# RWKV's triangular inverse with squares moved by transfers alone and masked products, and ScalarE's table set for logarithm and exponential asked for ahead of norms

## The chip, the cores and the metric

The kernel runs on one core of one Trainium2 chip. A core has TensorE (matrix products), VectorE, ScalarE (activations, by function tables that are loaded as sets) and GpSimd as compute engines, each with its own queue of instructions in a fixed order; SyncE (SP) issues most of the DMA transfers. Engines wait for each other by semaphores. The metric is the time of one launch on the device in microseconds.

## The reference

A step of a decoder trunk of two layers, on 512 prompt tokens and 8 x 8 sample tokens, with width 1024. Each layer mixes tokens with four recurrent mixers of four heads each (HGRN2, GLA, RWKV-7, RetNet), gates their results, and adds a gated feed-forward network:

```python
h = RMSNorm(x); P = h @ W_in[l]
o_b = mixer_b(P_b)                     # hg, gl, rw, rt: 256 wide each
x = x + W_out[l](sum_b sigmoid(G_b) * (o_b @ W_branch[l, b]))
x = x + SwiGLU(RMSNorm(x))

def rwkv7_recurrence(r, log_w, k, v, kk, a, s0):
    def step(S, inp):
        kS = jnp.einsum('bhk,bhkv->bhv', kk_t, S)
        S = (jnp.exp(lw_t)[..., None] * S
             - (a_t * kk_t)[..., None] * kS[..., None, :]
             + k_t[..., None] * v_t[..., None, :])
        return S, jnp.einsum('bhk,bhkv->bhv', r_t, S)
```

RMSNorm, the mixers' head norms (`_head_rms`, RWKV's `_head_layernorm` and the normalised `kk`) all need a reciprocal square root.

## The kernel before

Tokens lie along the free axis, 576 of them, worked on as two halves of 288. A weight product is three fp16 matmuls per k tile, high and low parts of both operands (lines 241 to 243, tile `pb`); the weights arrive as float32 and are split by ScalarE (line 228) and VectorE (line 229), 512 columns at a time. The input projection, the mixers and the gates run interleaved: `mix` (line 1623) goes through units of weight products in a hand-made order and advances a Python generator for each mixer at a pace (table `PACE`); a scheduler then fixes the order on each engine from what is ready. TensorE so has weight products beside the chain of small steps of the mixers.

**RWKV.** Nine chunks of 64 tokens are evaluated in closed form. `rwkv_pair` (line 669) works on two of the four heads at once, head pair 0 or 1, so there are two in each layer and four in the run. It makes the triangular matrices of a chunk, products `gps` (line 733) of `rw_br` and `rw_ab` (written at line 723), which VectorE masks into U (`rw_ub`, line 737): 128 partitions (two heads x 64 tokens) by 9 chunks by 128 columns, block diagonal by heads. Meanwhile `bps` (line 754) waits for the bonus term `rn` (line 750).

`rwkv_inverse` (line 894) then inverts the unit triangular I + U:

- GpSimd multiplies U by the constant `diag16` into W, so that only the 16x16 squares on the diagonal remain (line 901), and VectorE adds the eight squares of a row up into a compact `uc` of 16 columns (line 903);
- eight transfers on SP's queue carry `uc` to DRAM (`d1`, line 907), and one brings it back with a square per partition (`pp`, line 909). VectorE inverts the 72 squares by 15 steps of substitution, with a result `wp` that goes to `d2` (line 924) and in eight transfers back to `wc` (line 927);
- VectorE spreads `wc` over W with the mask (line 938). Then, for two groups of four chunks, the blocks of 32 and 64 follow: W is transposed (`itt`, line 946), multiplied by a part of U (`imu`, U masked for the level by line 932; product `ixp`, line 950), copied to SBUF by ScalarE (line 952), multiplied by W (`iyp`, line 960), and subtracted from W by VectorE (line 962).

In the same stretch VectorE runs HGRN2's and GLA's levels: scores of a chunk are built level by level from `lk` (line 1111) and `qt` (line 1122) with TensorE's product `lvp` (line 1026) and a predicated copy (line 1137).

**Reciprocal square roots.** All are made on ScalarE as exp(-0.5 ln(.)). The compiler puts a load of a table set ahead of an activation whose function is not in the set that is loaded. The places are `rstd` (RMSNorm, lines 444 and 445; called by `norm_half`), `head_rms_out` (HGRN2, GLA, RetNet, lines 515 and 516, behind the product `hps`), `rw_gen` (RWKV's norm, lines 657 and 658, behind `vps`) and `rwkv_pair` (the norm of `kk`, lines 694 and 695, behind `kps`). Around them ScalarE computes tanh for gates and sigmoids (lines 498, 630, 1458, 1540), exponentials for decays (line 1110) and silu in the feed-forward (line 1779). A gate's product with its branch is `gu` (line 1550).

Of the kernel before, what the change touches and what calls it, by code (L numbers as in the profile page):

```python
# [62 lines left out]
def host_constants():  # L63

    f = []
# [26 lines left out]
    for m in (16, 32):  # L92
        up = ((s2[:, None] // (2 * m) == s2[None, :] // (2 * m)) & (s2[:, None] // m % 2 == 0)
              & (s2[None, :] // m % 2 == 1)).astype(np.float32) * same
        put(f"rw_l{m}", up)
    put("diag16", (p[:, None] // 16 == p[None, :] // 16).astype(np.float32))
    c = np.arange(128)
# [77 lines left out]
class Net:  # L175
# [250 lines left out]
    def sq_acc(self, k, half, last=False):  # L426
# [8 lines left out]
        elif not last:  # L435
            nc.vector.tensor_tensor(self.acc[half], self.acc[half], sq, op=ADD)

    def rstd(self, half):

        nc = self.nc  # L440
        ps = self.psum("g", [128, HW], "rps")
        nc.tensor.matmul(ps, self.cf("ones"), self.acc[half], start=True, stop=True)
        r = self.t("e", [128, HW], "rstd")
        nc.scalar.activation(r, ps, AF.Ln, scale=1.0 / D, bias=self.eps[:, 0:1])
        nc.scalar.activation(r, r, AF.Exp, scale=-0.5)
        return r

    def norm_half(self, name, l, half, keep=False):


        nc = self.nc
        hs = slice(half * HW, half * HW + HW)
        if half == 0:
            self.h = [self.t("u", [128, 2, T], f"h{k}", F16) for k in range(KT)]
        self.norm_tiles(name, l, half, self.rstd(half), [x[:, hs] for x in self.x], keep)

# [47 lines left out]
    def head_rms_out(self, o, g, wcol, name):  # L504
# [3 lines left out]
        for j in range(2):  # L508
            sq = self.t("gs", [128, T], "hsq")
            nc.scalar.activation(sq, o[j], AF.Square)  # L510
            yield
            for t0, n in ((0, HW), (HW, HW)):
                ps = self.psum("g", [128, n], "hps")
                nc.tensor.matmul(ps, self.cf("head"), sq[:, t0:t0 + n], start=True, stop=True)
                nc.scalar.activation(sq[:, t0:t0 + n], ps, AF.Ln, scale=1.0 / 64, bias=self.eps[:, 0:1])
# [120 lines left out]
    def rw_gen(self, l):  # L636
# [4 lines left out]
        for j in range(2):  # L641
# [6 lines left out]
            for hs in part:  # L648
# [3 lines left out]
                nc.scalar.copy(O[:, hs], ps)  # L652
                yield
            for hs in part:
                ps = self.psum("r", [128, HW], "vps")
                nc.tensor.matmul(ps, self.cf("head"), sq[:, hs], start=True, stop=True)
                nc.scalar.activation(sq[:, hs], ps, AF.Ln, scale=1.0 / 64, bias=self.eps[:, 1:2])
# [11 lines left out]
    def rwkv_pair(self, l, j, lw):  # L669
# [16 lines left out]
        rn = tmp("rn")  # L686
        yield
        for hs in halves:
            ps = self.psum("r", [128, HW], "kps")
# [204 lines left out]
    def rwkv_inverse(self, U):  # L894
# [3 lines left out]
        ub = U.rearrange("p c h s -> p c (h s)")  # L898
        dg = self.cf("diag16").rearrange("p (g t) -> p g t", t=16)
        W = self.t("rd", [128, 9, 128], "rw_w")  # L900
        nc.gpsimd.tensor_tensor(W, ub, self.cf("diag16")[:, None, :].to_broadcast([128, 9, 128]), op=MUL)
        uc = self.t("r2", [128, 9, 16], "rw_uc")
        nc.vector.tensor_reduce(uc, W.rearrange("p c (g t) -> p c t g", t=16), axis=mybir.AxisListType.X, op=ADD)
        d1 = self.dr.tile([8, 9, 16, 16], F32, tag="d1", name="rw_d1")
        d2 = self.dr.tile([8, 9, 16, 16], F32, tag="d2", name="rw_d2")
        for g in range(8):
            nc.sync.dma_start(out=d1[g].rearrange("c s t -> s c t"), in_=uc[16 * g:16 * g + 16])
        pp = self.t("r1", [72, 16, 16], "rw_pp")
# [15 lines left out]
        nc.sync.dma_start(out=d2.rearrange("g c s t -> (g c) s t"), in_=wp)  # L924
        wc = self.t("r2", [128, 9, 16], "rw_wc")
        for g in range(8):
            nc.sync.dma_start(out=wc[16 * g:16 * g + 16], in_=d2[g].rearrange("c s t -> s c t"))
        n = 4

        def part(c0, m):  # L930
            mu = self.t("r2", [128, n, 128], "imu")
            nc.vector.tensor_tensor(mu, ub[:, c0:c0 + n], self.cf(f"rw_l{m}")[:, None, :].to_broadcast([128, n, 128]),
                                    op=MUL)
            return mu
        mu = part(0, 16)
        for _ in range(3):
            yield
        nc.vector.tensor_tensor(W.rearrange("p c (g t) -> p c g t", t=16),
                                wc[:, :, None, :].to_broadcast([128, 9, 8, 16]),
                                dg[:, None].to_broadcast([128, 9, 8, 16]), op=MUL)  # L940
        for c0 in (0, 4):
            w0 = W[:, c0:c0 + n]
            w = w0
            for m in (16, 32):
# [4 lines left out]
                for i in range(n):  # L949
                    nc.tensor.matmul(ps[:, i], mu[:, i], tt[:, i], start=True, stop=True)  # L950
                xx = self.t("r2", [128, n, 128], "ixx")
                nc.scalar.copy(xx, ps)
                if m == 16:
                    mu = part(c0, 32)
                elif c0 == 0:
                    mu = part(4, 16)
                yield
                ps = self.psum("r", [128, n, 128], "iyp")
                for i in range(n):
                    nc.tensor.matmul(ps[:, i], xx[:, i], w[:, i], start=True, stop=True)  # L960
                w2 = self.t("r2", [128, n, 128], "iw") if m == 16 else w0
                nc.vector.tensor_tensor(w2, w, ps, op=SUB)
                w = w2
                yield
# [994 lines left out]
```

## Time and profile before

| | |
|---|---|
| median of 3 runs | 2194.13 us (2193.98 to 2196.09) |
| the profiled execution | 2198.27 us, span 2196.5 us |
| TensorE busy | 2032.3 us |
| VectorE busy | 1622.8 us |
| ScalarE busy | 1080.3 us |
| GpSimd busy | 643.7 us |

The span runs from the first to the last instruction of the profiled execution; its own time adds what lies around it. Busy time does not count waiting. A timeline's row gives start, duration, engine, line, operation, output and inputs, and in brackets the idle time before it with what ended it. Line numbers are those of the kernel before.

### The profile page before, as it was taken

Reading aid. Unit: us, or ns where it says so; the run is one execution under the profiler, and the core shown is the slowest. Engines: PE = TensorE matmul, PEld = TensorE weight load, DVE = VectorE, ACT = ScalarE, POOL = GpSimd, SP = SyncE. Lnnn points to the kernel's source line nnn. Section 1 sums busy time; section 2 is a strip of 40 time slices with the busy share of each in tenths; the row PEclk is TensorE's granted clock in tenths of the full one; section 3 lists DMA queues with packets and bytes.
Section 4 is the critical chain, followed back from the end, with each engine's and each line's share of the span. In section 5 each row is a group of like instructions: output and inputs, shape, how many; then the busy total and the mean of one; then the engine's idle time right before and its main releaser. Section 6 shows DMA issues by size and latency. Waiting matters only on the chain.

```text
span 2196.5 us, 42364 instructions
## 1 busy us (share of the span) xinstructions
PE 2032.3 (93%) x15754; PEld 1608.8 (73%) x15754; DVE 1622.8 (74%) x3409; ACT 1080.3 (49%) x2524; POOL 643.7 (29%) x889
## 2 busy tenths in 40 slices
PE   7989999998998899999999899989999989999998
PEld 5767786786776677777777678768777767777776
DVE  7889667768786899863488986586778778998441
ACT  6554546345555555432466355453645455544332
POOL 2223222146541534310012142213464225332000
PEclk9999999999999999999999999999999999999999
DMA  6312224334545455453421222242354544554431
GB/s 182 84 42 63 59 59 110 78 84 106 132 121 170 101 141 132 111 145 99 125 66 50 55 64 59 74 111 62 85 133 112 154 130 116 136 137 107 125 107 51
DMA packets 381275, 223.75 MB, mean 102 GB/s; under 512 B 60675, under 2 KB 361275, under 8 KB 381069
## 3 DMA queue, kind: packets, MB, share of 16 engines
q1 hardware_dynamic: 365516, 192.73, 31.3%
q0 software_dynamic: 15552, 28.32, 7.4%
q8 instruction: 124, 2.03, 0.4%
q14 instruction: 83, 0.67, 0.1%
HBM read 173.72 MB, written 16.59 MB: 87 GB/s over the span
## 4 chain that ended last, share of the span: by engine, by line
PE 49%; DVE 25%; ACT 8%; issue 8%; DMA 5%; POOL 3%; SPq 1%; DVEq 0%; ACTq 0%; POOLq 0%
PE pb L243 5%; PE pb L242 5%; PE pb L241 5%; PE xb L243 4%; PE xb L242 4%; PE xb L241 4%; PE fsS L1736 2%; PE fsS L1735 2%; PE fsS L1734 2%; DVE hA L1704 2%; DVE whl L229 2%; DVE fy L1781 2%; DVE hS L1704 2%; DVE sc L1750 2%; DVE su L1750 2%
## 5 line engine op out<-in xcount | busy, mean ns | idle before, releaser
L241 PE MATMUL pb<-h,whl 128*128 128x288 f16 (+1 forms) x1504 | 434.6, 289 | 4.4 <-ACT whl L228 2.1
L243 PE MATMUL pb<-h,whl 128*128 128x288 f16 (+1 forms) x1504 | 434.2, 289 | 3.2 <-DVE whl L229 3.1
L242 PE MATMUL pb<-h,whl 128*128 128x288 f16 (+1 forms) x1504 | 434.6, 289 | 0.6 <-DVE h L465 0.4
L229 DVE SCALAR_TENSOR_TENSOR whl<-raw,whl 128x512 f16<-128x512 f32 (+1 forms) x352 | 253.6, 730 | 130.5 <-ACT whl L228 128.8
L243 PEld LDWEIGHTS <-whl 128*128 128x128 f16 (+1 forms) x2784 | 274.9, 99 | 86.5 <-issue 11.6
L242 PEld LDWEIGHTS <-whl 128*128 128x128 f16 (+1 forms) x2784 | 275.1, 99 | 85.0 <-issue 10.7
L241 PEld LDWEIGHTS <-whl 128*128 128x128 f16 (+1 forms) x2784 | 276.7, 99 | 76.1 <-issue 3.6
L228 ACT ACTIVATE whl<-raw 128x512 f16<-128x512 f32 (+1 forms) x352 | 213.0, 617 | 165.2 <-PE pb L243 50.6
L243 PE MATMUL xb<-fa,whl 128*128 128x288 f16 x704 | 201.3, 286 | 0.0
L242 PE MATMUL xb<-fa,whl 128*128 128x288 f16 x704 | 201.3, 286 | 0.0
L241 PE MATMUL xb<-fa,whl 128*128 128x288 f16 x704 | 201.3, 286 | 0.0
L1734 PE MATMUL fsS<-st,hS 128*128 128x288 f16 x456 | 132.5, 291 | 6.5 <-ACT hS L1703 6.5
L1734 PE MATMUL fsA<-h,hA 128*128 128x288 f16 x432 | 124.2, 288 | 9.4 <-DVE gu L1550 8.4
L1736 PE MATMUL fsS<-st,hS 128*128 128x288 f16 x456 | 132.5, 291 | 0.4 <-DVE hS L1704 0.3
L1735 PE MATMUL fsS<-st,hS 128*128 128x288 f16 x456 | 132.5, 291 | 0.0
L1736 PE MATMUL fsA<-h,hA 128*128 128x288 f16 x432 | 124.3, 288 | 0.2
L1735 PE MATMUL fsA<-h,hA 128*128 128x288 f16 x432 | 124.3, 288 | 0.0
L1703 ACT ACTIVATE hS<-sraw 128x512 f16<-128x512 f32 x130 | 79.8, 623 | 63.6 <-POOL sraw L1718 42.4
L1734 PEld LDWEIGHTS <-hS 128*128 128x128 f16 x864 | 85.5, 99 | 34.6 <-ACT hS L1703 12.6
L1704 DVE SCALAR_TENSOR_TENSOR hS<-sraw,hS 128x512 f16<-128x512 f32 x130 | 103.2, 798 | 9.1 <-ACT hS L1703 8.1
L1736 PEld LDWEIGHTS <-hS 128*128 128x128 f16 x864 | 85.7, 99 | 24.6 <-DVE hS L1704 2.4
L1735 PEld LDWEIGHTS <-hS 128*128 128x128 f16 x864 | 85.6, 99 | 22.8
(489 smaller groups left out, 5207.6 us busy)
## 6 DMA issues: line engine op xcount, KB each, us to landing
raw<-in_w_in SPq DMA_DIRECT2D x208, 256.0 KB
sraw<-in_w_ffn_in SPq DMA_DIRECT2D x40, 512.0 KB
raw<-in_w_ffn_out SPq DMA_DIRECT2D x80, 256.0 KB
raw<-in_w_ffn_in SPq DMA_DIRECT2D x78, 256.0 KB
sraw<-sraw POOLq DMA_DIRECT2D x40, 256.0 KB, 3.7
x<-xd SPq DMA_DIRECT2D x32, 288.0 KB
raw<-sraw POOLq DMA_DIRECT2D x34, 256.0 KB, 3.3
sraw<-in_w_in SPq DMA_DIRECT2D x32, 256.0 KB
```

Source lines behind the costliest of these rows:

```text
L228: nc.scalar.activation(hl[:, 0, :n], raw[:, :n], AF.Copy, scale=WS)
L229: nc.vector.scalar_tensor_tensor(hl[:, 1, :n], raw[:, :n], WS, hl[:, 0, :n], op0=MUL, op1=SUB)
L241: nc.tensor.matmul(ps, wh, hi, start=i == 0, stop=False)
L242: nc.tensor.matmul(ps, wh, lo, start=False, stop=False)
L243: nc.tensor.matmul(ps, wl, hi, start=False, stop=i == len(ks) - 1)
L1703: nc.scalar.activation(hl[:, 0], a, AF.Copy, scale=WS)
L1704: nc.vector.scalar_tensor_tensor(hl[:, 1], a, WS, hl[:, 0], op0=MUL, op1=SUB)
L1734: nc.tensor.matmul(ps, w[a][:, 0, k], hi, start=k == 0, stop=False)
L1735: nc.tensor.matmul(ps, w[a][:, 0, k], lo, start=False, stop=False)
L1736: nc.tensor.matmul(ps, w[a][:, 1, k], hi, start=False, stop=k == 3)
L1750: nc.vector.tensor_tensor(o, a, p, op=op)
L1781: nc.vector.scalar_tensor_tensor(y, u, PH * AS, sg, op0=MUL, op1=MUL)
```

## The change

The inverse. GpSimd fills W with zeros and U isn't masked. The eight transfers to `d1` read the 16x16 squares on U's diagonal from U itself, and the eight from `d2` write the inverted squares onto W's diagonal; `uc`, `wc`, the reduction, the spread and `diag16` go. The products `ixp` take U unmasked, ScalarE's copy negates, and the last product is written into W by a copy that is predicated by the level's mask, in place of masks on U and a subtraction.

The tables. A method `table` asks for a table set at its place in the order, which the scheduler keeps. It asks for the set with both functions ahead of `rstd`'s product, `hps` and `vps`, for the set "natural_log" ahead of `kps`, and behind `rstd` for the set of silu or of exp.

```diff
+    def table(self, name="natural_log_exp_and_others"):
+
+        self.tc.keep_in_program_order(self.nc.scalar.preload_act_table_set(name))
+
     def rstd(self, half):
         ps = self.psum("g", [128, HW], "rps")
+        self.table()
         nc.tensor.matmul(ps, self.cf("ones"), self.acc[half], start=True, stop=True)
...
-        self.norm_tiles(name, l, half, self.rstd(half), [x[:, hs] for x in self.x], keep)
+        r = self.rstd(half)
+        self.table("silu_and_others" if keep else "exp_and_others")
+        self.norm_tiles(name, l, half, r, [x[:, hs] for x in self.x], keep)
...
@@ head_rms_out, for each j, ahead of both hps
+            self.table()
@@ rw_gen, ahead of both vps
+            self.table()
@@ rwkv_pair, ahead of both kps
+        self.table("natural_log")
...
@@ rwkv_inverse
         ub = U.rearrange("p c h s -> p c (h s)")
-        dg = self.cf("diag16").rearrange("p (g t) -> p g t", t=16)
         W = self.t("rd", [128, 9, 128], "rw_w")
-        nc.gpsimd.tensor_tensor(W, ub, self.cf("diag16")[:, None, :].to_broadcast([128, 9, 128]), op=MUL)
-        uc = self.t("r2", [128, 9, 16], "rw_uc")
-        nc.vector.tensor_reduce(uc, W.rearrange("p c (g t) -> p c t g", t=16), axis=mybir.AxisListType.X, op=ADD)
+        nc.gpsimd.memset(W, 0.0)
...
         for g in range(8):
-            nc.sync.dma_start(out=d1[g].rearrange("c s t -> s c t"), in_=uc[16 * g:16 * g + 16])
+            b = slice(16 * g, 16 * g + 16)
+            nc.sync.dma_start(out=d1[g].rearrange("c s t -> s c t"), in_=ub[b, :, b])
...
-        wc = self.t("r2", [128, 9, 16], "rw_wc")
         for g in range(8):
-            nc.sync.dma_start(out=wc[16 * g:16 * g + 16], in_=d2[g].rearrange("c s t -> s c t"))
+            b = slice(16 * g, 16 * g + 16)
+            nc.sync.dma_start(out=W[b, :, b], in_=d2[g].rearrange("c s t -> s c t"))
...
-        def part(c0, m):
-            mu = self.t("r2", [128, n, 128], "imu")
-            nc.vector.tensor_tensor(mu, ub[:, c0:c0 + n], self.cf(f"rw_l{m}")[:, None, :].to_broadcast([128, n, 128]),
-                                    op=MUL)
-            return mu
-        mu = part(0, 16)
         for _ in range(3):
             yield
-        nc.vector.tensor_tensor(W.rearrange("p c (g t) -> p c g t", t=16),
-                                wc[:, :, None, :].to_broadcast([128, 9, 8, 16]),
-                                dg[:, None].to_broadcast([128, 9, 8, 16]), op=MUL)
...
-                    nc.tensor.matmul(ps[:, i], mu[:, i], tt[:, i], start=True, stop=True)
+                    nc.tensor.matmul(ps[:, i], ub[:, c0 + i], tt[:, i], start=True, stop=True)
                 xx = self.t("r2", [128, n, 128], "ixx")
-                nc.scalar.copy(xx, ps)
-                if m == 16:
-                    mu = part(c0, 32)
-                elif c0 == 0:
-                    mu = part(4, 16)
+                nc.scalar.activation(xx, ps, AF.Copy, scale=-1.0)
...
-                w2 = self.t("r2", [128, n, 128], "iw") if m == 16 else w0
-                nc.vector.tensor_tensor(w2, w, ps, op=SUB)
-                w = w2
+                mk = self.cf(f"rw_l{m}").bitcast(I32)
+                nc.vector.copy_predicated(w, mk[:, None, :].to_broadcast([128, n, 128]), ps)
```

What stands where in the built kernels (the changed kernel's own line numbers differ by some 10; `L439` is the method `table`). First VectorE around U of head pair 0 in layer 0, before:

```order
242 L739 TENSOR_TENSOR rw_ar<-gps,cst 128x64
243 L229 SCALAR_TENSOR_TENSOR whl<-raw,whl 128x512
244 L423 SCALAR_TENSOR_TENSOR gl_lg<-cst,gl_lg 128x128 x2
245 L903 TENSOR_REDUCE rw_uc<-rw_w 128x144
246 L1071 TENSOR_TENSOR gs<-gkv,cst 128x256
247 L1107 TENSOR_TENSOR le_2010<-hg_f 128x256
248 L1074 SCALAR_TENSOR_TENSOR gs<-gs,glb 128x128 x2
249 L423 SCALAR_TENSOR_TENSOR gl_lg<-cst,gl_lg 128x128
250 L1111 TENSOR_TENSOR lk_2011<-hg_k,le_2010 128x256
251 L1122 TENSOR_TENSOR qt_568<-hg_q,le_2010 64x2x64 x2
```

and now:

```order
245 L748 TENSOR_TENSOR rw_ar<-gps,cst 128x64
246 L228 SCALAR_TENSOR_TENSOR whl<-raw,whl 128x512
247 L422 SCALAR_TENSOR_TENSOR gl_lg<-cst,gl_lg 128x128 x2
248 L422 SCALAR_TENSOR_TENSOR gl_lg<-cst,gl_lg 128x64
249 L1063 TENSOR_TENSOR gs<-gkv,cst 128x256
250 L1099 TENSOR_TENSOR le_2009<-hg_f 128x256
251 L1066 SCALAR_TENSOR_TENSOR gs<-gs,glb 128x128 x2
252 L1103 TENSOR_TENSOR lk_2010<-hg_k,le_2009 128x256
253 L1114 TENSOR_TENSOR qt_568<-hg_q,le_2009 64x2x64 x2
```

The reduction is gone from ahead of `qt`, one scan of `gl_lg` stands earlier, and two more rows stand ahead of row 245 than ahead of row 242 before: a split of weights and another scan of `gl_lg`.

ScalarE at HGRN2's head norm of layer 0 (`hsq` is what the norm is made of, `le` a decay's exponential, `ixx` a copy in the inverse), before:

```order
235 L515 ACT_TABLE_LOAD
236 L515 ACTIVATE hsq<-hps,eps 128x288 x2
237 L952 COPY ixx<-ixp 128x512
238 L516 ACT_TABLE_LOAD
239 L516 ACTIVATE hsq<-hsq 128x576
240 L1110 ACTIVATE le_2988<-le_2988 128x16x4 x2
241 L515 ACT_TABLE_LOAD
242 L515 ACTIVATE hsq<-hps,eps 128x288 x2
243 L1110 ACT_TABLE_LOAD
244 L1110 ACTIVATE le_3027<-le_3027 128x32x2
245 L516 ACTIVATE hsq<-hsq 128x576
```

and now:

```order
230 L439 ACT_TABLE_LOAD
231 L1102 ACTIVATE le_2921<-le_2921 128x8x8 x2
232 L227 ACTIVATE whl<-raw 128x512
233 L493 ACTIVATE cur<-pb 128x288
234 L439 ACT_TABLE_LOAD
235 L522 ACTIVATE hsq<-hps,eps 128x288 x2
236 L949 ACTIVATE ixx<-ixp 128x512
237 L523 ACTIVATE hsq<-hsq 128x576
238 L227 ACTIVATE whl<-raw 128x512
239 L1102 ACTIVATE le_2977<-le_2977 128x16x4
240 L522 ACTIVATE hsq<-hps,eps 128x288 x2
241 L1102 ACTIVATE le_2977<-le_2977 128x16x4
```

Two loads stand ahead of the first `hsq` from `hps`, none from there to the second.

ScalarE ahead of a gate's tanh (`gth`) in layer 0, now; `kvb` and `rxv` are copies in RWKV:

```order
505 L803 COPY kvb_581<-rw_v 64x64
506 L439 ACT_TABLE_LOAD
507 L1450 ACT_TABLE_LOAD
508 L1450 ACTIVATE gth<-pb 128x288
509 L828 COPY rxv<-xvp 128x256
```

Two loads stand in a row, where one stood ahead of the same tanh (line 1458) before.

## Rows read from the trace of the kernel before

**Rows 1.** busy time of each engine over the whole span, with its instruction count.

```profile
PE 2032.3 (93%) x15754; PEld 1608.8 (73%) x15754; DVE 1622.8 (74%) x3409; ACT 1080.3 (49%) x2524; POOL 643.7 (29%) x889
```

**Rows 2.** shares of the chain of work that ended last.

```profile
PE 49%; DVE 25%; ACT 8%; issue 8%; DMA 5%; POOL 3%; SPq 1%; DVEq 0%; ACTq 0%; POOLq 0%
```

**Rows 3.** what TensorE waited for: total us, times, longest us.

```profile
PE lvp L1026 <- DVE qt L1122: 19.9, 18, 3.6
...
PE gps L733 <- DVE rw_ab L723: 7.6, 2, 4.1
...
PE bps L754 <- DVE rn L750: 6.8, 2, 3.6
...
PE lvp L1026 <- ACT hsq L515: 5.3, 2, 2.6
...
PE fsA L1734 <- DVE gu L1550: 8.4, 6, 2.4
```

**Rows 4.** VectorE in order of time, head pair 0 of layer 0: start, us.

```profile
146.79 3.08 DVE L229 SCALAR_TENSOR_TENSOR whl<-raw,whl 128x512 f16<-128x512 f32 x1
...
150.44 2.05 DVE L903 TENSOR_REDUCE rw_uc<-rw_w 128x144 f32<-128x1152 f32 x1
...
154.25 0.58 DVE L1122 TENSOR_TENSOR qt<-hg_q,le 64x128 f32<-64x128 f32 x2
```

**Rows 5.** TensorE there, and in layer 1; idle time before it in brackets.

```profile
154.98 1.19 PE L1026 MATMUL lvp<-qt,lk 128*128 128x128 f32 x4 [3.63 <-DVE qt L1122]
...
1228.48 0.68 PE L1026 MATMUL lvp<-qt,lk 128*128 128x128 f32 x4 [3.63 <-DVE qt L1122]
```

**Rows 6.** groups by line: busy us in all, mean ns of one.

```profile
L901 POOL TENSOR_TENSOR rw_w<-rw_ub,cst 128x1152 f32<-128x1152 f32 x4 | 11.6, 2894 | 37.3 <-DVE rw_ub L737 37.3
...
L229 DVE SCALAR_TENSOR_TENSOR whl<-raw,whl 128x512 f16<-128x512 f32 x332 | 244.9, 744 | 128.4 <-ACT whl L228 126.7
...
L932 DVE TENSOR_TENSOR imu<-rw_ub,cst 128x512 f32<-128x512 f32 x16 | 11.0, 688 | 3.9 <-PE ixp L950 3.9
...
L938 DVE TENSOR_TENSOR rw_w<-rw_wc,cst 128x1152 f32<-128x1152 f32 x4 | 5.4, 1359 | 0.2 <-issue 0.2
...
L962 DVE TENSOR_TENSOR iw<-rw_w,iyp 128x512 f32<-128x512 f32 x8 | 5.5, 689 | 2.6 <-PE iyp L960 2.6
...
L1137 DVE COPY_PREDICATED sc<-lev,lvp 128x256 f32<-128x256 int32 x112 | 57.8, 516 | 13.7 <-PE lvp L1026 12.9
```

**Rows 7.** stretches: start:end, length, busy us (count) of PE PEld DVE ACT POOL, PEclk.

```profile
133.50:156.00 22.50, 18.18 (x132) 15.06 (x133) 22.02 (x47) 7.60 (x24) 4.83 (x8) 0.89 0.24 61
...
376.00:397.00 21.00, 15.15 (x105) 11.67 (x106) 19.89 (x35) 8.37 (x17) 3.53 (x3) 0.92 0.39 101
...
1291.00:1310.00 19.00, 15.74 (x105) 12.07 (x104) 14.74 (x26) 13.75 (x26) 6.85 (x15) 0.91 0.25 66
...
1448.00:1475.00 27.00, 19.75 (x134) 15.54 (x132) 23.24 (x40) 11.39 (x22) 4.62 (x6) 0.87 0.36 94
```

**Rows 8.** ScalarE in order of time at HGRN2's head norm, layer 0.

```profile
217.50 1.28 ACT L515 ACT_TABLE_LOAD   x1
...
222.47 1.28 ACT L515 ACT_TABLE_LOAD   x1
...
223.76 0.89 ACT L515 ACTIVATE hsq<-hps,eps 128x288 f32<-128x288 f32 x2
...
224.67 1.28 ACT L1110 ACT_TABLE_LOAD   x1
```

**Rows 9.** VectorE in order of time, head pair 1 of layer 0.

```profile
384.82 3.71 DVE L229 SCALAR_TENSOR_TENSOR whl<-raw,whl 128x512 f16<-128x512 f32 x2
...
389.20 2.07 DVE L903 TENSOR_REDUCE rw_uc<-rw_w 128x144 f32<-128x1152 f32 x1
```

**Rows 10.** a GpSimd memset beside VectorE's split, in order of time.

```profile
444.21 0.31 POOL L1160 MEMSET gkh<- 128x256 f32 x1
444.27 0.68 DVE L229 SCALAR_TENSOR_TENSOR whl<-raw,whl 128x512 f16<-128x512 f32 x1
```

More of the change, by code (lines that the diff above doesn't have):

```diff
@@ L95, in host_constants @@
         put(f"rw_l{m}", up)
-    put("diag16", (p[:, None] // 16 == p[None, :] // 16).astype(np.float32))
     c = np.arange(128)
@@ L924, in rwkv_inverse @@
         nc.sync.dma_start(out=d2.rearrange("g c s t -> (g c) s t"), in_=wp)
-        wc = self.t("r2", [128, 9, 16], "rw_wc")
         for g in range(8):
-            nc.sync.dma_start(out=wc[16 * g:16 * g + 16], in_=d2[g].rearrange("c s t -> s c t"))
+            b = slice(16 * g, 16 * g + 16)
+            nc.sync.dma_start(out=W[b, :, b], in_=d2[g].rearrange("c s t -> s c t"))
         n = 4
-        def part(c0, m):
-            mu = self.t("r2", [128, n, 128], "imu")
-            nc.vector.tensor_tensor(mu, ub[:, c0:c0 + n], self.cf(f"rw_l{m}")[:, None, :].to_broadcast([128, n, 128]),
-                                    op=MUL)
-            return mu
-        mu = part(0, 16)
         for _ in range(3):
             yield
-        nc.vector.tensor_tensor(W.rearrange("p c (g t) -> p c g t", t=16),
-                                wc[:, :, None, :].to_broadcast([128, 9, 8, 16]),
-                                dg[:, None].to_broadcast([128, 9, 8, 16]), op=MUL)
         for c0 in (0, 4):
-            w0 = W[:, c0:c0 + n]
-            w = w0
+            w = W[:, c0:c0 + n]
             for m in (16, 32):
```

## The prediction

> **What bounds the kernel now.** I read the busy times first: TensorE works 2032.3 us of a span of 2196.5 us, so all its idle time together is 164.2 us; VectorE is at 74% and ScalarE at 49% [rows 1]. The chain that ended last is half TensorE and a quarter VectorE [rows 2]. So no amount of saved work on VectorE or ScalarE counts by itself: it counts where TensorE stands still for it. The list of TensorE's waits says where that is [rows 3]. Four of its entries hang on work that the change touches: the level products `lvp` that wait for `qt` (19.9 us over 18 waits, two of them 3.6 us), `gps` that waits for `rw_ab` (7.6 us over 2), `bps` that waits for `rn` (6.8 us over 2), and `lvp` behind HGRN2's head norm (5.3 us over 2). Each has one instance per layer, so what is found in layer 0 is counted twice. Last I read those stretches in order of time. In the two RWKV stretches of layer 0, VectorE is busy 22.02 of 22.5 us and 19.89 of 21 us while TensorE is not [rows 7]: there VectorE is the bound, and a microsecond off it is worth up to one.
>
> **The inverse, head pair 0.** GpSimd's masked copy of U takes 2.9 us, four times per run [rows 6]. It does not run beside VectorE for nothing: the split (line 229) that meets it takes 3.08 us where the mean of its form is 0.74 [rows 4, 6], so VectorE loses 2.3 us. The reduction behind it takes 2.05 [rows 4]. Both stand ahead of the `qt` for which TensorE waits 3.63 us in each layer [rows 5]. The change puts a memset for the mask and drops the reduction: 4.4 us off VectorE ahead of that `qt`. The new order lets back in one scan more and moves one split up, which by their durations is about 1 us, so 3.0 of the 3.63 us go: **-6.0 us** for two layers. Between what bounds: nothing (the split is held by the memset as it was by the copy, and the rest moves) and the whole 7.3. For the memset I take no hold at all: a smaller memset of 0.31 us starts 0.06 us ahead of a split that then takes 0.68 us, its normal time [rows 10]. If it held the split through, it would take back at most the 2.3 us above, four times, of which two lie on TensorE's path.
>
> **Behind it in pair 0.** Four masks of 0.69 us and the spread of the squares, 1.36 us, leave VectorE in each inverse [rows 6]: 16 x 0.69 + 4 x 1.36 = 16.4 us in the run, half of it in pair 0, where TensorE waits for VectorE in pieces of 0.6 to 1 us that are part of the 19.9 [rows 3]. I take 1 us per layer: **-2.0 us**, bounds 0 and -4.5. In pair 1 the same work lies beside long matrix products, and I take nothing. The masked product in the subtraction's place is a predicated copy of 128x512. A predicated copy of half that size takes 0.52 us in the mean, a subtraction of the whole size 0.69 [rows 6]; so it costs between 0 and +0.35 us more each, 16 times, half of them in pair 0, and TensorE waits for few of them: bounds 0 to +2, taken as 0. The transfers keep their number, eight out and eight back on SP's queue, and start earlier, with the reduction gone from ahead of them.
>
> **Pair 1.** The same two things stand between `rw_ab` and the `rn` for which `bps` waits: the pair of splits takes 3.71 us where twice 0.74 is normal, and the reduction 2.07 [rows 6, 9]. That is 4.3 us out of VectorE's way, against waits of 6.8 us over the two layers [rows 3], 3.4 each. In the new order one more split stands there, so 3.6 us net: both waits go, **-6.8 us**. Against it: ahead of the same chain ScalarE now loads a table before `rw_sg` and another before `re`. The first falls into time in which ScalarE waits for VectorE, so I cost it at nothing; if that cover is gone it is 1.28 us per layer. The second delays `re`, and with it `rw_ab`, for which TensorE already waits 7.6 us over two layers [rows 3]: 2 x 1.28 = **+2.6 us** [rows 8].
>
> **The tables at the norms.** At HGRN2's head norm ScalarE loads four tables within 9 us, 1.28 us each [rows 8]: logarithm, exponential, logarithm, exponential, while TensorE waits 2.6 us for the second logarithm [rows 3]. In the new order two loads stand there, both before the first logarithm, and none between. The two that go, 2.57 us, cover the wait: **-5.3 us** for two layers, bounds -3 and -5.3 (the extra load for the next tanh comes where ScalarE waits anyway). In the feed-forward norm one load less stands in the second half of each layer, at most 1.28 us each; TensorE's wait there also hangs on VectorE, so I take half, **-1.3 us**. The first half is behind other products, and RetNet's and GLA's norms are not waited for.
>
> **Where loads are added.** By the listings of the two built kernels the change does not lower the count in the whole program: 71 loads against 61, as some of the preloads do not replace a load but precede another one. The added ten are 10 x 1.28 = 12.8 us of ScalarE. Twice per layer a preload stands directly ahead of another load, in front of the tanh of the gates, and TensorE waits for the product of gate and branch (`gu`) 8.4 us in six waits [rows 3]. One of the two pairs per layer I place on that path: **+2.6 us**, bounds 0 and +5.1.
>
> First the row on what a load costs: the logarithm starts at 223.76, 1.29 us after its load started [rows 8], so a load holds ScalarE for its 1.28 us and nothing more. The Trainium skill ("ScalarE: Activation LUTs", What ACT_TABLE_LOAD costs) states 1283 ns and about 1380 ns of drain on top, 2.66 us for a switch. By that, the ten added loads would be 26.6 us of ScalarE, and the forecast some 3 us higher; the trace does not agree on the drain, so I go by the trace.
>
> **The clock.** In the four stretches the granted clock is 0.89, 0.92, 0.91 and 0.87 [rows 7]: it falls to the lower of its two levels (1.2 instead of 2.4 GHz) for some microseconds after TensorE stood still. The loss is 0.11 x 22.5 + 0.08 x 21 + 0.09 x 19 + 0.13 x 27 = 9.4 us. Two of the stretches keep another wait of over 3 us (the earlier `qt`, and `rw_ab`), so I take a third back, **-3.1 us**, bounds 0 and -6.7.
>
> **Sum.** -6.0 - 2.0 - 6.8 + 2.6 - 5.3 - 1.3 + 2.6 - 3.1 = -19.3 us. The profiled execution took 2198.3 us with a span of 2196.5; the median of the runs is 2194.1, 0.2% less. A difference of 19 us is the same for both, so the forecast is 2194.1 - 19.3 = 2175 us, 0.9% less.
>
> **Rivals.** *The waits only move.* VectorE's order around pair 0 is full of work for TensorE; what is taken out lets TensorE reach the next `lvp`, `gop` or `bps` sooner, and it stands there instead. For it: the 18 waits for `qt`, of which only two are the long ones [rows 3]. Against it: in pair 1 TensorE is busy 15.15 of 21 us with weight products that don't wait for the chain [rows 7], so it has work to fill the time with. Then only the head norm's 5.3 us and some 2 of the rest are left, against the +5.2 us of added loads: 2194.1 - 2 = 2192 us. *The table loads decide it.* The point is ScalarE's path to `rw_ab` and to the gates: if it is ScalarE and not VectorE that is late there, then what leaves VectorE in pair 1 is worth nothing and each added load is paid in full, with its place kept by an order that can't move it. Price: 12.8 us for ten loads, less the 5.3 at the head norm and 2 in pair 0: 2194.1 + 5.5 = 2200 us. For it: TensorE already waits for `rw_ab`, and for the gates. Against it: ScalarE is busy only 8.37 of 21 us in pair 1's stretch [rows 7]. *All of it comes.* At the outer bounds -7.3 - 4.5 - 6.8 - 5.3 - 2.6 - 6.7 + 2.6 = -30.6: 2163 us. *The change does not do what it says*: the preloads don't replace loads at all at the head norm, because the compiler puts its own behind them. The listing of the built kernel speaks against it there, and for it at the gates; then 5.3 us less: 2180, inside the forecast's own range.
>
> **How the numbers follow.** The forecast, from 2168 to 2185, has 0.55; all of it, 2160 to 2168, 0.10; less than the forecast but still a gain, 2185 to 2189.7, 0.09; the waits only move, 2190 to 2198, 0.14; the loads decide, above 2198.5, 0.12. A difference of 0.2%, 4.4 us, is about what a measurement of this kernel can tell from none. That gives faster 0.74, same 0.14, slower 0.12. The range leaves out the lower half of the full gain and the slower case: 2164 to 2197.
>
> **What would show it.** In the new trace: the split that meets the memset takes about 0.7 us, and no wait of 3.6 us for `qt` stands near 151 or 1225 (pair 0); `bps <- rn` falls from 6.8 to under 1 us, and `gps <- rw_ab` rises from 7.6 to about 10; `lvp <- hsq` is gone; `fsA <- gu` rises from 8.4 to about 11; the granted clock of the stretch at HGRN2's head norm in layer 1 is 1.00. Wrong would be: waits for `qt` that stay at 19.9 us in sum, a split still at 3 us beside the memset, a predicated copy of over 1 us, or a total TensorE idle time near 164 us.

## The result and the profile after

The changed kernel takes 2171.6 us in the median of four runs (2170.0 to 2174.8), the kernel before 2194.9 in the same set. The ratio is 0.9889, with an interval of 0.9877 to 0.9902: 1.1% or 24 us faster. The forecast was 2175 us. The profile after, as its page gives it, the line with the span and the one with the busy times:

```profile
span 2173.0 us, 42394 instructions
...
PE 2028.8 (93%) x15754; PEld 1603.7 (74%) x15754; DVE 1587.5 (73%) x3385; ACT 1089.7 (50%) x2534; POOL 630.3 (29%) x889
```

TensorE's idle time is 2173.0 - 2028.8 = 144.2 us, against 164.2 [rows 1]: 20.0 us less. Its busy time is 3.5 us less with the same number of products, which I put down to the clock (mean granted clock 0.982 against 0.981). Together they are the 23.5 us by which the span is shorter. What TensorE waited for, by the list of its waits (total us, times, longest us), to be set beside [rows 3]:

```profile
PE lvp L1018 <- DVE qt L1114: 10.8, 14, 2.8
PE fsA L1726 <- DVE gu L1542: 10.0, 7, 3.0
PE xvp L825 <- DVE rws L877: 9.0, 6, 3.0
PE gps L742 <- DVE rw_ab L732: 5.4, 2, 2.8
...
PE fb L241 <- POOL h L471: 4.0, 2, 2.0
...
PE xps L859 <- ACT rw_o L831: 3.5, 2, 1.8
...
PE bps L763 <- DVE rn L759: 3.0, 2, 2.3
```

The waits for `qt` fell from 19.9 to 10.8 us, those for `rn` from 6.8 to 3.0. The wait for HGRN2's `hsq`, 5.3 us before, has no row any more. `rw_ab` did not go where the prediction put it: it fell from 7.6 to 5.4. `gu` rose from 8.4 to 10.0, but a second profile of the same kernel (e12 below) has 8.3 for `gu` and 4.5 for `gop` behind `vz`, where this one has 10.0 and 3.1; so a single profile does not show changes of 1 to 2 us in these two entries. The other entries above come back in e12 within 0.6 us. The rows for GpSimd's `h` and for `xps` had no counterpart of that size before.

VectorE behind the last part of U in head pair 0, layer 0, in order of time (start, us), and TensorE's product behind `qt`, to be set beside [rows 4, 5]:

```profile
146.46 0.46 DVE L746 TENSOR_TENSOR rw_ub<-gps,cst 64x64 f32<-64x64 f32 x2
...
147.10 0.68 DVE L228 SCALAR_TENSOR_TENSOR whl<-raw,whl 128x512 f16<-128x512 f32 x1
147.69 0.92 DVE L422 TENSOR_TENSOR_SCAN gl_lg<-cst,gl_lg 128x128 f32<-128x128 f32 x3
...
150.24 0.58 DVE L1114 TENSOR_TENSOR qt<-hg_q,le 64x128 f32<-64x128 f32 x2
```

```profile
150.96 0.68 PE L1018 MATMUL lvp<-qt,lk 128*128 128x128 f32 x4
```

The split takes 0.68 us in place of 3.08, the reduction is gone, `qt` is done by 150.8 where it took until 154.8 before, and the product has no idle time in brackets where it had 3.63. The memset is not even near the split: GpSimd does it 24 us earlier, since it needs nothing of U. So whether it would hold a split that it met was not put to the test here.

```profile
122.88 1.06 POOL L909 MEMSET rw_w<- 128x1152 f32 x1
```

And the group of the predicated copies (busy us in all, mean ns of one) shows 0.73 us for 128x512, against 0.69 of the subtraction [rows 6]:

```profile
L955 DVE COPY_PREDICATED rw_w<-cst,iyp 128x512 f32<-128x512 int32 x16 | 11.6, 726 | 3.9 <-PE iyp L953 3.8
```

ScalarE at HGRN2's head norm, layer 0, in order of time, beside [rows 8]; and the product `lvp` that waited there:

```profile
211.13 1.28 ACT L439 ACT_TABLE_LOAD   x1
...
213.66 1.28 ACT L439 ACT_TABLE_LOAD   x1
214.95 0.89 ACT L522 ACTIVATE hsq<-hps,eps 128x288 f32<-128x288 f32 x2
...
217.48 0.99 ACT L522 ACTIVATE hsq<-hps,eps 128x288 f32<-128x288 f32 x2
```

```profile
218.12 0.67 PE L1018 MATMUL lvp<-qg,lk 128*128 128x256 f32 x2
```

Both loads stand ahead of the first logarithm, and from there to the second there is none. The product starts without idle time. The clock, by stretches that answer to [rows 7] (busy us with counts of PE, PEld, DVE, ACT, POOL, then PEclk):

```profile
133.50:152.00 18.50, 17.53 (x131) 14.62 (x132) 17.54 (x46) 8.12 (x24) 2.88 (x8) 0.91 0.20 47
365.00:388.00 23.00, 18.02 (x129) 14.13 (x127) 18.98 (x39) 9.77 (x21) 2.63 (x7) 0.93 0.35 88
1272.00:1292.00 20.00, 19.11 (x143) 15.40 (x142) 16.10 (x32) 14.71 (x34) 6.85 (x16) 1.00 0.22 59
1430.00:1452.00 22.00, 18.50 (x132) 14.40 (x131) 18.98 (x39) 9.72 (x21) 2.75 (x7) 0.92 0.35 89
```

At the head norm of layer 1 it is 1.00, from 0.91. In pair 1 of layer 1 it is 0.92, from 0.87; in the other two it hardly moved. In e12, the same kernel again, it is 1.00, 0.93, 1.00 and 1.00 in the same four stretches (the last two start some 4 us earlier there): only the second and the third come out alike in both profiles.

### The profile page after: what moved, and what is told of

The parts are those of the page before. It is cut to its first block, busy times and chain, and to the rows that moved or that the text cites. A ratio compares the mean times of both kernels' runs of the same rounds, so it can differ in the third digit from the quotient of the medians.

```text
span 2173.0 us, 42394 instructions
## 1 busy us (share of the span) xinstructions
PE 2028.8 (93%) x15754; PEld 1603.7 (74%) x15754; DVE 1587.5 (73%) x3385; ACT 1089.7 (50%) x2534; POOL 630.3 (29%) x889
## 4 chain that ended last, share of the span: by engine, by line
PE 50%; DVE 22%; ACT 9%; issue 8%; DMA 6%; POOL 2%; SPq 1%; DVEq 0%; ACTq 0%; POOLq 0%
PE pb L242 5%; PE pb L241 5%; PE pb L240 5%; PE xb L241 4%; PE xb L242 4%; PE xb L240 4%; PE fsS L1728 2%; PE fsS L1726 2%; PE fsS L1727 2%; DVE fy L1773 2%; DVE hA L1696 2%; DVE hS L1696 2%; DVE sc L1742 2%; DVE su L1742 2%; PE lvp L1018 2%
## 5 line engine op out<-in xcount | busy, mean ns | idle before, releaser
L228 DVE SCALAR_TENSOR_TENSOR whl<-raw,whl 128x512 f16<-128x512 f32 (+1 forms) x352 | 243.1, 699 | 138.9 <-ACT whl L227 137.0
L1726 PEld LDWEIGHTS <-hS 128*128 128x128 f16 x864 | 85.5, 99 | 34.9 <-ACT hS L1695 12.9
L1696 DVE SCALAR_TENSOR_TENSOR hA<-sraw,hA 128x512 f16<-128x512 f32 x110 | 96.6, 888 | 13.1 <-ACT hA L1695 13.1
L1728 PEld LDWEIGHTS <-hS 128*128 128x128 f16 x864 | 85.3, 99 | 24.8 <-DVE hS L1696 2.4
```

The lines of the kernel that those rows point to most:

```text
L228: nc.vector.scalar_tensor_tensor(hl[:, 1, :n], raw[:, :n], WS, hl[:, 0, :n], op0=MUL, op1=SUB)
L1696: nc.vector.scalar_tensor_tensor(hl[:, 1], a, WS, hl[:, 0], op0=MUL, op1=SUB)
L1726: nc.tensor.matmul(ps, w[a][:, 0, k], hi, start=k == 0, stop=False)
L1728: nc.tensor.matmul(ps, w[a][:, 1, k], hi, start=False, stop=k == 3)
```

## The experiments

e1 to e4 were made on one chip and e5 to e12 on another; the kernel before takes 2200.6 to 2201.5 us beside them. Each is given as its ratio to the kernel before on the same chip, and in us as that share of 2194. "Idle" is the span less TensorE's busy time, from each run's page. The kernel before was profiled only beside the result (idle 164.2 us); e6 and e7, which take as long as it does, have 164.5 and 163.6. Below the overview the runs are grouped by what they ask.

| run | what it is | ratio (95%) | us | idle us |
|---|---|---|---|---|
| the change | | 0.9889 (0.9877 to 0.9902) | -24 | 144.2 |
| e1 | the inverse alone | 0.9942 (0.9922 to 0.9962) | -13 | 155.4 |
| e2 | all table requests alone | 0.9963 (0.9949 to 0.9977) | -8 | 151.0 |
| e3 | the change, GpSimd's mask kept | 0.9919 (0.9896 to 0.9942) | -18 | 146.7 |
| e4 | the change, a reduction kept | 0.9890 (0.9870 to 0.9910) | -24 | 143.3 |
| e5 | HGRN2's head norm's request alone | 0.9969 (0.9955 to 0.9983) | -7 | 156.1 |
| e6 | the request for the norm of `kk` alone | 0.9998 (0.9989 to 1.0008) | 0 | 164.5 |
| e7 | the requests that add loads, alone | 1.0007 (0.9991 to 1.0023) | +2 | 163.6 |
| e8 | the change without those | 0.9896 (0.9881 to 0.9910) | -23 | 145.5 |
| e9 | the requests around `rstd` alone | 0.9993 (0.9981 to 1.0005) | -2 | 156.2 |
| e10 | the change without the one at `vps` | 0.9893 (0.9876 to 0.9910) | -23 | 142.9 |
| e11 | the change without GLA's and RetNet's | 0.9888 (0.9872 to 0.9905) | -25 | 145.3 |
| e12 | the change again | 0.9893 (0.9875 to 0.9911) | -23 | 142.0 |

### The two parts by themselves (e1, e2)

e1 is the changed kernel with all calls of `table` taken out, e2 the kernel before with all of them put in.

```diff
 e1, against the changed kernel
-        self.table()                        # rstd; head_rms_out; rw_gen
-        self.table("silu_and_others" if keep else "exp_and_others")
-        self.table("natural_log")
```

> The changed inverse without any of the table requests. My theory: the two parts act in different places and add up. The inverse alone gives the pair 0 and pair 1 terms with their clock, about -13 us against the kernel before (0.994); the wait of lvp for HGRN2's hsq stays at about 5 us in two waits. Rival, the tables carry the gain: within 5 us of the kernel before. Second rival, the parts need each other (the gap at pair 1 only closes with both): less than 8 us. The wait of gps for rw_ab tells a further thing: 5.4 us as in the changed kernel if it comes from the inverse and its order, 7.6 us or more if the table requests shortened it.

> The table requests with the inverse as before. My theory: -5 us at HGRN2's head norm with up to 1.7 us of clock, -1 in the feed-forward norm, against +3 to +5 us where loads are added, so -2 to -5 us (0.998 to 0.999). In sum with the inverse alone it should give the -23 us of the whole change within 4 us. Rival, the tables carry the gain: -15 us or more. Rival, the ten added loads decide: slower than before by 2 us or more.

The inverse alone gives 13 us, the requests alone 8. Their sum, 21 us, agrees with the 24 of the whole within the intervals, so the parts need not be thought of as helping each other. e1's waits of TensorE:

```profile
PE lvp L1013 <- DVE qt L1109: 13.1, 17, 3.5
...
PE fsA L1721 <- DVE gu L1537: 11.5, 8, 2.9
...
PE gps L737 <- DVE rw_ab L727: 7.5, 2, 4.0
...
PE lvp L1013 <- ACT hsq L519: 5.2, 2, 2.6
```

HGRN2's `hsq` stays at 5.2 us, and `rw_ab` at 7.5, both as before: what happened to them in the change is the requests' doing. There is no row for `bps` and `rn` any more: the 6.8 us went entirely. `qt` fell by 6.8. But idle time fell by only 8.8 us in all, less than these two entries together (13.6): `gu` stands 3.1 us higher, of which up to 1.7 can be the difference between two profiles of one kernel, and several small waits 1 to 2 us higher (for instance `o0p`, a product in RWKV's later chain, 2.0 after 0.7). The requests came out at twice what I expected here, 8 us against 2 to 5, and idle time fell by 13.2 us.

### What in the inverse gives the time (e3, e4)

```diff
 e3, against the changed kernel
-        nc.gpsimd.memset(W, 0.0)
+        nc.gpsimd.tensor_tensor(W, ub, self.cf("diag16")[:, None, :].to_broadcast([128, 9, 128]), op=MUL)
 e4, against the changed kernel
         nc.gpsimd.memset(W, 0.0)
+        uc = self.t("r2", [128, 9, 16], "rw_uc")
+        nc.vector.tensor_reduce(uc, ub.rearrange("p c (g t) -> p c t g", t=16), axis=mybir.AxisListType.X, op=ADD)
```

e4 does a reduction whose result nothing reads.

> The changed kernel, but GpSimd fills W with U times diag16 as before in place of the memset. It puts back one thing, GpSimd's read of U beside VectorE. My theory: VectorE's split that meets it takes 3.1 to 3.7 us again, the first wait for qt behind it comes back with 1 to 2 us, and the time is +4 to +8 us against the changed kernel. Rival, the hold costs nothing since VectorE has slack by then: within 2 us of the changed kernel.

> The changed kernel with a reduction of U on VectorE at its old place, whose result nobody reads. My theory: 2.05 us of VectorE four times, ahead of qt and rn, of which TensorE waits for most: +4 to +8 us against the changed kernel, and with the run that keeps the mask it accounts for most of what the inverse gave. Rival, only the hold by GpSimd mattered: within 2 us of the changed kernel.

With the mask kept, GpSimd's product and VectorE in head pair 0 of layer 0:

```profile
147.69 2.63 POOL L910 TENSOR_TENSOR rw_w<-rw_ub,cst 128x1152 f32<-128x1152 f32 x1 [8.56 <-DVE rw_ub L747]
```

```profile
147.78 3.08 DVE L229 SCALAR_TENSOR_TENSOR whl<-raw,whl 128x512 f16<-128x512 f32 x1
...
153.32 0.58 DVE L1115 TENSOR_TENSOR qt<-hg_q,le 64x128 f32<-64x128 f32 x2
```

```profile
154.04 0.35 PE L1019 MATMUL lvp<-qt,lk 128*128 128x128 f32 x1 [2.34 <-DVE qt L1115]
```

The split starts 0.09 us after GpSimd's product and ends at 150.86, half a microsecond after it (150.32), as if it had begun only then. `qt` follows late, and the product `lvp` waits 2.34 us again, in both layers; the waits for `qt` are 14.7 us in sum, against 10.8 in the change, and those for `rn` 4.1 against 3.0. In head pair 1 of layer 1 GpSimd started just after the split, and the next instruction was held instead, a product of 128x288 that takes 0.45 us in the row behind it:

```profile
1452.59 3.12 POOL L910 TENSOR_TENSOR rw_w<-rw_ub,cst 128x1152 f32<-128x1152 f32 x1 [11.90 <-PE pb L243]
```

```profile
1452.54 0.68 DVE L229 SCALAR_TENSOR_TENSOR whl<-raw,whl 128x512 f16<-128x512 f32 x1
1453.14 2.88 DVE L1359 TENSOR_TENSOR rt_sw<-rt_sw,rt_sin 128x288 f32<-128x288 f32 x1
1455.94 0.45 DVE L1360 TENSOR_TENSOR rt_k<-rt_k,rt_cos 128x288 f32<-128x288 f32 x1
```

The run is 0.003 slower than the change, 6 to 7 us. The size is rough: the two intervals overlap at their ends, and taken as independent they leave 1 to 12 us for the difference; against e12, the change again, the difference is 0.0026, and the same working no longer tells it from none. Its idle time rose by only 2.5 us, its busy time by 7.6 (2036.4 against 2028.8, with the same products): the returned waits brought the lower clock back with them, or the profiled run happened to meet it more often; one profile cannot tell these apart.

With the reduction kept:

```profile
147.17 2.10 DVE L911 TENSOR_REDUCE rw_uc<-rw_ub 128x144 f32<-128x1152 f32 x1
...
151.31 0.58 DVE L1116 TENSOR_TENSOR qt<-hg_q,le 64x128 f32<-64x128 f32 x2
...
152.27 0.91 DVE L422 TENSOR_TENSOR_SCAN gl_lg<-cst,gl_lg 128x128 f32<-128x128 f32 x3
```

```profile
152.04 0.35 PE L1020 MATMUL lvp<-qt,lk 128*128 128x128 f32 x1 [0.82 <-DVE qt L1116]
```

It takes 2.10 us on VectorE and `lvp` waits 0.82 us, where it had no wait in the change. The time is that of the change within its interval: the first expectation fell, the rival stands. The rows say in part why it costs so little. The scheduler put the three scans of `gl_lg` (0.91 us) behind `qt` (152.27), where the change has them ahead of it (147.69), so `qt` starts only 1.07 us later (151.31 against 150.24). The waits for `qt` do come back in part, 13.6 us against 10.8, but TensorE's idle time as a whole does not (143.3 us against 144.2): other waits are shorter by as much. So of the two things that I added up, the hold by GpSimd is seen in the rows and costs some 6 us, with an interval that only just leaves out none; the reduction by itself costs less than these runs can tell (some 5 us).

That leaves about half of e1's 13 us without a run of its own. The masks and the spread that left VectorE, and the transfers that no longer wait for the mask and the reduction (the substitution's first instruction in pair 0 starts at 155.82 in the change and at 162.97 before), were not put back one by one.

### The requests one by one (e5, e6, e7, e9)

Each is the kernel before with some of the calls of `table`.

```diff
 e5, head_rms_out                        e6, rwkv_pair, ahead of kps
+            if name == "hg":             +        self.table("natural_log")
+                self.table()
 e7, head_rms_out and rw_gen             e9, rstd and norm_half
+            if name != "hg":             +        self.table()
+                self.table()             +        self.table("silu_and_others" if keep else "exp_and_others")
+            self.table()
```

> The kernel before with one edit: the table set with both functions is asked for ahead of hps at HGRN2's head norm alone. My theory: the waits of lvp for hsq (5.3 us in two) go, with the 1.2 us for ixp behind one of them, TensorE's idle time falls by 5 to 7 us, and the time by as much. That leaves 6 to 8 of the 13 us of idle time that the whole of the table requests took away for the other requests. Rival, the head norm is all of it: 12 us or more less idle time.

> The kernel before with one edit: the logarithm's set is asked for ahead of kps, RWKV's norm of kk. It adds 4 loads (67 against 63). By the step of my prediction that counts each load on ScalarE as later work, it costs 0 to +2.6 us. By the rival that grew out of the trace of the changed kernel (what counts is that the load leaves the stretch between kps and rn, where VectorE waits, and is done while TensorE and VectorE still work towards kps), it takes 2 to 5 us of TensorE's idle time away, among it 0.7 us at the first long wait for qt in each layer (3.49 to 2.80), although ScalarE is busy 5.1 us more.

> The kernel before with the requests that add loads: GLA's and RetNet's head norms and RWKV's norm (vps), 73 loads against 63. My prediction's term for the added loads is +2.6 us at the gates and +2.6 at rw_ab, so +5 us and more of idle time, in gu and rw_ab. Rival: the ten loads lie beside TensorE's weight products or replace loads on the chain, and idle time moves by under 2 us. Second rival, as the difference left over by the other two suggests: these requests too give 3 us or more.

> The kernel before with the requests around rstd alone (both functions ahead of the product, silu's or exp's set behind it); the number of loads stays at 63. What the other runs leave over of the 13 us of idle time that all the table requests take away is 4 to 5 us. My theory: it is here, in fb, TensorE's first products of the feed-forward, whose waits for fsg (4.1 us) and h (6.6 us) fall by 7 to 8 us in sum and come back with 4 us as waits for GpSimd's h; time -3 to -5 us. My prediction's term was -1.3 us. Rival: the rest comes from no single request but from the order as a whole, then this run shows less than 2 us.

e5 behaved as expected: 7 us, 8.1 us of idle time, and no row for `hsq`.

e6 came out at nothing, between -2 and +2 us, and with an idle time as before. The second theory's 2 to 5 us of idle time is not there; the lower half of the first theory's cost is not ruled out. Its waits for `qt`:

```profile
PE lvp L1032 <- DVE qt L1128: 17.4, 19, 3.6
```

They fell by 2.5 us, 1.4 of it at the first long wait of each layer (3.49 and 3.48 before, 2.80 and 2.81 now), as the second theory wanted. Why the idle time did not fall with them is open: `gu` rose by 1.6 us and `vz` by 1.5, but two profiles of the changed kernel differ by 1.7 and 1.4 in the same entries.

e7 adds ten loads, 12.8 us of ScalarE, and the time is +2 us with an interval from -2 to +5. Its waits are not the ones that I priced:

```profile
PE fsA L1742 <- DVE gu L1558: 8.9, 6, 2.6
...
PE gps L741 <- DVE rw_ab L731: 6.0, 2, 3.4
...
PE xps L858 <- ACT rw_o L830: 3.3, 2, 1.8
```

`gu`, for which I took +2.6 us, is up by 0.5. `rw_ab`, for which I took +2.6 as well, is down by 1.6. `xps`, a product of RWKV's later chain, waits 3.3 us, and `yps`, which waits for `rx`, 4.4 in place of 1.9; `xvp`, which waits for `rws` in the same chain, waits 9.0 in place of 11.8. The idle time as a whole is that of the kernel before (163.6 against 164.2).

e9 has an idle time 8.0 us smaller, but a measured time only 2 us smaller, with an interval that reaches zero:

```profile
PE fb L242 <- POOL h L472: 3.7, 2, 2.0
...
PE fb L242 <- DVE h L472: 2.2, 3, 1.0
...
PE fb L241 <- ACT h L471: 2.0, 2, 1.0
```

In the kernel before the same products waited:

```profile
PE fb L242 <- DVE h L465: 6.6, 8, 1.8
...
PE fb L241 <- ACT fsg L1779: 4.1, 2, 2.1
```

The waits for `fsg` are gone, those for VectorE's `h` fell from 6.6 to 2.2, and 5.7 us of waits for the other engines' `h` stand in their place. That is 4.8 us; the rest of the idle time that this profile lacks is in small waits elsewhere. Its busy time is 5.3 us above that of the kernel before, whose profile comes from the other set; with the same products, that is clock. So the trace alone would have given this request too much; the timed runs put it between a loss of 1 us and a gain of 4.

### A leaner set of requests (e8, e10, e11, e12)

```diff
 e8, against the changed kernel: both; e11: the first; e10: the second
+            if name == "hg":             # head_rms_out
                 self.table()
-            self.table()                 # rw_gen, ahead of vps
```

> The changed kernel without the requests at GLA's and RetNet's head norms and at RWKV's norm: 65 loads against 73. If added loads cost what I forecast, it is 3 to 5 us faster than the changed kernel (about 0.987 of the kernel before) and the best version so far; gu's wait falls from 10.0 us to 8.5. Rival, if those requests give time rather than cost it: 2 to 5 us slower than the changed kernel (0.990 to 0.991).

> The changed kernel without the request ahead of vps (71 loads against 73). The lean run took this request and those of GLA's and RetNet's head norms out together and lost what they shorten (rw_ab, rws) against what they lengthen (bps, yps, xps). If the request ahead of vps is the one that lengthens xps and yps in RWKV's chain, this is up to 4 us faster than the changed kernel; if it is the one that shortens rw_ab and rws, up to 4 us slower; within 2 us if neither.

> The changed kernel without the requests at GLA's and RetNet's head norms (67 loads against 73), the other half of the lean run's edit. Here the two preloads that stand directly ahead of a gate's tanh are gone, so gu's wait should fall from 10.0 to about 8.5 us by my prediction's term for the gates (2.6 us). Rival: that term was empty, ScalarE has slack at the gates, and gu stays at about 10.

> The changed kernel itself, on the chip of these runs, so that the runs of this call can be set against it directly: 0.9889 of the kernel before within 0.002.

All four agree within their intervals. Nothing that these runs can tell (3 to 4 us) is won by leaving out the loads that precede another load, and nothing is lost. e11's trace, without the two preloads that stand ahead of a gate's tanh in each layer:

```profile
PE fsA L1727 <- DVE gu L1543: 10.7, 7, 2.9
PE gps L743 <- DVE rw_ab L733: 7.5, 2, 4.0
```

`gu` waits 10.7 us, no less than in the change, and `rw_ab` is back at 7.5. e12, the change again, differs from the change's first profile in `gu` and `vz`:

```profile
PE fsA L1726 <- DVE gu L1542: 8.3, 6, 3.0
...
PE gop L1048 <- DVE vz L1144: 4.5, 6, 2.1
```

So `gu`, between 8.3 and 11.5 us in all these profiles, does not follow the number of loads: it is 8.6 in e2, with all ten added, and 11.5 in e1, with none. At one of the two pairs of loads in each layer the added one even falls into time in which ScalarE waits: in the change it starts at 555.32, and the next load only at 559.48, after 2.88 us of waiting for VectorE.

The rows of pair 1 in layer 0 say why `rw_ab` moves. In the kernel before, one of VectorE's two products `rw_br` meets a product of GpSimd and takes 1.93 us:

```profile
369.53 1.84 POOL L702 TENSOR_TENSOR rn<-rb,rw_sg 128x576 f32<-128x576 f32 x1 [5.75 <-DVE ksq L700]
```

```profile
370.06 1.93 DVE L715 TENSOR_TENSOR rw_br<-rw_r,re 128x576 f32<-128x576 f32 x1
```

In the change a load asked for GLA's head norm stands on ScalarE ahead of `re`. VectorE waits for that norm, and comes to `rw_br` after GpSimd's product has ended (362.65):

```profile
360.33 1.28 ACT L439 ACT_TABLE_LOAD   x1
```

```profile
361.25 1.40 POOL L711 TENSOR_TENSOR rn<-rb,rw_sg 128x576 f32<-128x576 f32 x1 [6.49 <-DVE ksq L709]
```

```profile
364.65 0.75 DVE L724 TENSOR_TENSOR rw_br<-rw_r,re 128x576 f32<-128x576 f32 x1
```

So the load that I had priced as a delay of `re` also took an instruction out of a hold. All profiles divide in the same way: this `rw_br` takes 1.34 us in the mean of its four in the kernel before, e1, e5, e6, e8, e9 and e11, where the wait for `rw_ab` is 7.0 to 7.7 us, and 0.75 in the change, e2, e3, e4, e7, e10 and e12, where it is 5.4 to 6.2. No run has this one load by itself.

What the requests at GLA's and RetNet's norms take away comes back behind it. In e8 and e11, without them, `rw_ab` and `rws` wait 20.3 us together, and `rn`, `yps` behind `rx` and `xps` behind `rw_o` 0.2 us or less; in the change, e10 and e12 the first two wait 14.4 to 15.3 and the other three 9.7 to 10.3. No version here beats the change.

## Why the prediction came out right

The forecast of -19 us met -24, inside the range. The runs show that the main mechanisms hold, and that terms were wrong in opposite directions. By halves: for the inverse the three terms of waits are -14.8 us, and e1 measured -13 (-17 to -8); for the requests they are -5.3 - 1.3 + 5.2 = -1.4 us, and e2 measured -8 (-11 to -5). So it is the half of the requests in which the forecast gave too little.

**The inverse, pair 0 and pair 1.** Forecast -6.0 and -6.8 us, both in waits that are named. In e1 `qt` fell by 6.8 and `rn` by 6.8: the size is right. All but 0.3 us of the fall of `qt` is in the two long waits of pair 0 (3.63 to 0.37 in each layer). The working behind it was right in one half: the hold of VectorE by GpSimd's masked copy is shown by e3, which brings back a wait of 2.34 us in each layer and some 6 us of time (1 to 12). The other half, the reduction, was added to it as if VectorE's order stood still; e4 shows that it does not. For pair 1 the runs show less: `rn` waits 5.7 us in e2 and 3.0 in the change, and e3 and e4 bring back 1.1 and 0.5 us of that, where two profiles of the change differ by 0.3. What the prediction left out is the return: in e1's profile the idle time fell by 8.8 us where the two waits alone fell by 13.6, as `gu` and small waits took 5 us back. That was the first rival, the waits that only move, and in this profile it held for a third of the two waits; the time of e1 cannot tell the share.

**Behind pair 0.** Forecast -2.0. It is not to be seen: the waits for `qt` behind the long one, which I took as its sign, are 2.1 us in layer 0 before and 1.8 in e1, and 2.0 and 1.8 in layer 1.

**HGRN2's head norm.** Forecast -5.3 us, measured 7 (4 to 10) in e5. The step is right: two loads of 1.28 us stood between TensorE and the second logarithm, and without them the wait is gone, with 1.2 us of `ixp` behind it and some clock.

**The feed-forward norm.** Forecast -1.3, measured -2 (-4 to +1). No contradiction, but nothing at all is inside the interval too.

**The added loads.** This step failed: +2.6 us at `rw_ab` and +2.6 at the gates. I had placed the loads on paths that TensorE waits for, from the order alone. e7 has all ten of them and costs 2 us at most likely (-2 to +5), `rw_ab` waits less in it, and e8 and e11, which take out eight and six of them, are no faster. At `rw_ab` the step took the delay of `re` and left out what the delay does: VectorE's `rw_br` no longer meets GpSimd's product, takes 0.75 us in place of 1.93, and `rw_ab` fell by 2.2 us where I had +2.6. At the gates nothing is to be seen: `gu` reads 10.0 and 8.3 in two profiles of the change, and e1, which has no request at all, has the highest value (11.5). The second rival, that the loads decide it, falls by the same runs.

**`rn` in pair 1.** The check "under 1 us" failed: 3.0 us in the change and 2.7 in e12. It holds in e1, e8 and e11, where the list has no row for it, so the requests at GLA's and RetNet's norms gave some 3 us of it back, more than they took off `rw_ab` (7.5 to 5.4).

**The clock.** Forecast -3.1 us, and TensorE's busy time is 3.5 us less. The sum agrees; the places cannot be checked one by one. Only the head norm's 1.00 stands in both profiles of the change; pair 0 of layer 0 has 0.91 in one and 1.00 in the other, against 0.89 before, and pair 1 of layer 1 has 0.92 and 1.00, against 0.87. Between these two profiles the busy time moves by 1.4 us (2028.8 and 2030.2), so a part of the agreement is luck.

**The sum.** -19.3 was a good number by a cancellation, which is luck: the added loads were 5 us too dear, and the returned waits in the inverse, some 5 us in e1's profile, were not priced. With both put right the sum would still be near -20; the 4 us from there to the change's -24 no run assigns. What the five single requests and parts give by themselves (-13, -7, 0, +2, -2) adds up to -20 us, the change to -24, and the intervals are wide enough for both. The counts of loads in the prediction, 61 and 71, leave out two of each kernel; the listings have 63 and 73, and the difference of ten is right.

## What to carry to other kernels

Where GpSimd reads SBUF beside a loaded VectorE, look at the VectorE instruction that meets it before anything else: 2.4 us were lost there in an instruction of 0.7, four times, and a memset that ran 24 us ahead of the split was in nobody's way. A table load counts by where it stands, not by the number of loads: two loads in each layer, taken out from between a product and its next use, gave 7 us, ten put in at other places cost less than these runs can tell. A load can even help, where the delay moves an instruction out of another engine's way. And when an instruction leaves a busy engine, the order of the others changes with it, so price the wait that is named and then take something off for the waits that appear behind it; here it was a third of the two named waits, in one profile. Profile the same kernel twice before reading an entry of 1 or 2 us.

## What the runs showed of the hardware

A VectorE instruction that meets GpSimd's masked product is held until that is done, and it is whichever comes next: in e3 a split (3.08 us) where GpSimd started first; where the split had started just before, the instruction behind it, 2.88 us in place of 0.45, and there GpSimd's product itself took 3.12 us in place of 2.63. A smaller product of GpSimd, 128x576 in 1.84 us, held `rw_br` in the same way (1.93 us in place of 0.75). The Trainium skill ("SBUF — State Buffer", 🔬 SBUF: two separate sides) describes this as a port pair that one of the two holds for a whole instruction, when VectorE reads two operands from SBUF and GpSimd reads SBUF too; the traces agree, for both orders, by these numbers.

A predicated copy of 128x512 from PSUM took 0.73 us, hardly more than the subtraction of that size (0.69), though the copy of 128x256 under line 1137 takes 0.52 in the mean [rows 6].

A table load that is asked for takes 1.28 us like one that the compiler puts in, and the activation behind it starts 0.01 us after its end (213.66 and 214.95 above), so here a request cost ScalarE no more than the load.
